# The last pair's softmax division moved from the probabilities to the mixed values

## The chip, the cores and the metric

The kernel runs on one NeuronCore of a Trainium2 chip. The metric is the device time of one execution in microseconds (us). Runs of the kernel before lie between 1137.45 and 1139.55 us, with a median of 1137.94 us over three.

## The reference

One decoder layer on 1024 tokens of width 1024, all in float32. RMSNorm of x feeds one combined input projection. Sixteen heads of width 64 follow: eight with a sliding window, sink logits and ALiBi (group A), and eight with forgetting attention (group B), whose logit gets `c[t] - c[s]` from a running sum of log forget gates. The output projection with a residual comes next, then RMSNorm and an MLP with a squared ReLU. What matters here is the end of group B:

```python
sc = jnp.where(causal, sc + bias, -jnp.inf)
p = jax.nn.softmax(sc, axis=-1)
return jnp.einsum('bhqs,bshd->bqhd', p, v)
```

A softmax is an exponential divided by its row sum. The row sum belongs to the query, so the division can stand on the probabilities (query by key) or on the mixed values (query by head width), with the same outcome up to rounding.

## The kernel before, in words

Products in float32 are made of three products of a rounded part and a remainder (`hi`, `lo`), and stationary tiles are 128 by 128. The order of work is: input projection and group A, then the eight group B heads in four pairs (p = 0 to 3), with the projections of the next pair and, from the third pair on, the first half of the output projection as fillers between them; then the second half of the output projection; then the MLP (`up`, `down`), which takes from about 503 us to the end.

A pair is made of eight units (`heads_b`), one for each head h and each pair of query blocks qp (256 queries). The order of qp is 0, 2, 1, 3 for the first head, and 1, 3, 0, 2 for the second head of the last pair. A unit has two parts:

- `scores_b` makes for each of its two query blocks i the negated logits (TensorE, tile `spb`), adds the forget bias and takes the running minimum (VectorE, L626, tile `sb`), and exponentiates (ScalarE, L632), which also gives the row sum.
- `mix_b`, called two units later (DEPTH = 2), turns the probabilities by TensorE transposes into `tpb` (L662), moves them to SBUF as a rounded part (ScalarE, L359, `pth`) and a remainder (VectorE, L360, `ptl`), and multiplies them with the values into `pvb`. The values' rounded part and remainder sit side by side in the stationary tile, so that `pvb` has two halves of 64 partitions, which must be added: ScalarE copies the upper half to `tmpb` (L677), and VectorE adds the lower half to it (L679, `mtb`).

For the first three pairs the probabilities stay undivided. The row sums are collected in `dn_b`, and `split_mix` divides the mixed values later, after a round through DRAM (L565). The last pair makes no such round trip: the probabilities themselves are divided, with a reciprocal of one column (L639) and a multiplication of the whole row of up to 1024 keys, on VectorE for query blocks 2 to 7 (L641) and on GpSimd for blocks 0 and 1 (L643). The result of `mix_b` is then split at once into `mh[7]` and `ml[7]`, the last operand of the output projection (`mix`, ScalarE L75 and VectorE L78).

Beside the last pair run `out_first` (first half of the output projection, one call for each of eight output columns, tiles `po`, `wos`, `xt`), `split_mix(6)` with its loads and stores, and the loads of the divided earlier pairs (`load_mix`, tile `mix<-mixs_d`). After the last unit's scores the program makes products of the first output column with operands 4 to 6, and, when the last unit is mixed, with operand 7.

The engines take their instructions in order. That order is written by a planner, which places instructions by priority on a simulated timeline: program order, with scores, preparations and weight splits pulled forward by an offset (`high_priority`), and fillers held behind the score of a given unit (`issue_after`, `PACE`). Buffers are rings: two for `tpb`, `pvb`, `spb`, `pth`, `ptl` and `mtb`, one for `tmpb`. A tile of a ring is taken again once all that touched it has ended.

Of the kernel before, what the change touches and what calls it, by code (L numbers as in the profile page):

```python
# [8 lines left out]
F32 = mybir.dt.float32  # L9
# [3 lines left out]
ALU = mybir.AluOpType  # L13
# [3 lines left out]
P = 128  # L17
# [4 lines left out]
HD = 64  # L22
# [31 lines left out]
def hybrid_layer(  # L54
# [13 lines left out]
    nc = tc.nc  # L68
# [11 lines left out]
    def rsqrt(pool, out, t, shape, tag):  # L80
# [12 lines left out]
    ident = cp.tile([P, P], F32, name="ident")  # L93
    nc.gpsimd.memset(ident, 0.0)
    nc.gpsimd.affine_select(
        out=ident, in_=ident, pattern=[[-1, P]], compare_op=ALU.not_equal,
# [16 lines left out]
    for i in range(2):  # L113
        nc.vector.tensor_tensor(
            out=gqk[:, i : i + 1], in0=vec[:, 2 * i : 2 * i + 1],
            in1=vec[:, 2 * i + 1 : 2 * i + 2], op=ALU.mult,
# [487 lines left out]
    def scores_b(p, qp, h):  # L604
        q1, k1, k2, cb = heads[p, "q"][h], heads[p, "k1", h], k2_of[h], heads[p, "cb", h]
        probs = []
        for i in (2 * qp, 2 * qp + 1):
            nk = (i + 1) * P
            pr = ap2.tile(
                [P, S if i > 3 else 512], F32, tag="s" if i > 3 else "u", name="sb",  # L610
                bufs=NS if i > 3 else NU,
            )
            nm = ap2.tile([P, 4], F32, tag="nm", name="nmb", bufs=4)
            dn = ap2.tile([P, 4], F32, tag="dn", name="dnb", bufs=4)
            qs = q1[:, i * P : (i + 1) * P]
            for c in range((nk + 511) // 512):
                n = min(512, nk - c * 512)
                ne = max(n, 256)
                ks = slice(c * 512, c * 512 + ne)
                sp = pa.tile([P, 512], F32, tag="sc", name="spb", bufs=2)  # L620
                last = (c + 1) * 512 >= nk
                mm(sp[:, :ne], qs, k1[:, ks], True, False)
                mm(sp[:, :ne], qs, k2[:, ks], False, not last)
                if last:
                    pe = mm(sp[:, n - P : n], ident_b, mask_b, False, True)
                nc.vector.tensor_tensor_reduce(  # L626
                    out=pr[:, c * 512 : c * 512 + n], in0=sp[:, :n],
                    in1=cb[:, c * 512 : c * 512 + n], scale=1.0,
                    scalar=3e38 if c == 0 else nm[:, 0:1],
                    op0=ALU.add, op1=ALU.min, accum_out=nm[:, c : c + 1],  # L630
                )
            nc.scalar.activation(  # L632
                pr[:, :nk], pr[:, :nk], AF.Exp, scale=-1.0, bias=nm[:, c : c + 1],
                accum_out=dn_b[p % 2][:, h, i : i + 1] if p < 3 else dn[:, 0:1],
            )
            probs.append(pr)
            if p < 3:
                continue
            nc.vector.reciprocal(dn[:, 1:2], dn[:, 0:1])  # L639
            if i > 1:  # L640
                nc.vector.tensor_scalar_mul(pr[:, :nk], pr[:, :nk], dn[:, 1:2])  # L641
            else:
                nc.gpsimd.tensor_tensor(  # L643
                    out=pr[:, :nk], in0=pr[:, :nk],
                    in1=dn[:, 1:2].to_broadcast([P, nk]), op=ALU.mult,
                )
        marks.append(pe.ins)
        return probs

    def mix_b(probs, p, qp, h):  # L650
        r = slice(h * HD, (h + 1) * HD)
# [23 lines left out]
                mm(pvo, st, lv[:, :, 1 - par, :], False, diag and par == 1)  # L675
        tmp = ap2.tile([HD, 512], F32, tag="cmb", name="tmpb", bufs=1)
        nc.scalar.copy(tmp[:, :256], pv[HD:, :256])  # L677
        mt = ap2.tile([P, 256], F32, tag="mt", name="mtb", bufs=2)
        nc.vector.tensor_tensor(out=mt[r, :], in0=pv[:HD, :256], in1=tmp[:, :256], op=ALU.add)  # L679
        ms = slice(qp * 256, (qp + 1) * 256)  # L680
        if p < 3:
            nc.sync.dma_start(mix_d[4 + p, r, ms], mt[r, :])
# [562 lines left out]
```

## Time and profile before

| | us |
|---|---|
| median of three runs | 1137.94 |
| lowest, highest | 1137.45, 1139.55 |
| the profiled execution | 1135.57 |
| its span, first to last instruction | 1133.8 |
| TensorE busy (share of the span) | 1105.2 (97%) |
| VectorE busy | 767.8 (68%) |
| ScalarE busy | 574.4 (51%) |
| GpSimd busy | 383.4 (34%) |

The granted clock of TensorE is 0.998 of full speed over the span. Busy time of TensorE counts a matmul to its modelled end, and neighbours overlap: a group's mean of one is longer than the distance from one matmul to the next. Idle time in square brackets is that of the instruction's engine just before it, with the instruction that ended it. Line numbers are those of the kernel before; L71, L75 and L78 are helpers (`mm`, and the two halves of `split`), so tiles say what they work on. PE is TensorE, PEld its weight loads, DVE VectorE, ACT ScalarE, POOL GpSimd.

### The profile page before, as it was taken

The page shows a single profiled execution, that of the slowest core. Times are in us where ns is not written, and L with a number is a line of the kernel's source. Part 1 is how long each engine was busy: PE and PEld are TensorE (multiplying, and loading weights), DVE is VectorE, ACT ScalarE, POOL GpSimd, SP SyncE. Part 2 cuts the span into 40 slices and gives each one's busy share as a digit, 9 for nine tenths or more (in the row PEclk, how much of TensorE's full clock was granted, in tenths as well). Part 3 has the DMA queues.
Part 4 walks back from the last instruction along what each step waited for, and adds up shares of the span by engine and source line. Part 5 has one row for each costly group of instructions (what it writes and reads, how often), then busy time and mean ns, then how long its engine had stood idle before and what let it go on. Part 6 is the DMA issues. An engine that isn't in the chain of part 4 may idle for free.

```text
span 1133.8 us, 15566 instructions
## 1 busy us (share of the span) xinstructions
PE 1105.2 (97%) x5551; PEld 937.0 (83%) x5551; DVE 767.8 (68%) x1307; ACT 574.4 (51%) x1013; POOL 383.4 (34%) x342
## 2 busy tenths in 40 slices
PE   9999999989999999999999999999999999999998
PEld 8999987888997887787888887888888888888876
DVE  7476665766558577798867677856575877674493
ACT  5567567666557666545454534344443433333330
POOL 5751513345324634133332322222222222231241
PEclk9999999999999999999999999999999999999999
DMA  9311301355307647363554544335699786665441
GB/s 314 117 43 29 94 20 54 94 170 167 105 27 294 196 166 258 124 231 130 186 195 168 194 149 154 141 119 200 227 391 347 265 303 233 230 232 183 167 149 38
DMA packets 95710, 195.68 MB, mean 173 GB/s; under 512 B 7136, under 2 KB 19088, under 8 KB 95632
## 3 DMA queue, kind: packets, MB, share of 16 engines
q1 hardware_dynamic: 95488, 194.66, 49.0%
q8 instruction: 44, 0.72, 0.3%
q14 instruction: 34, 0.28, 0.1%
q10 hardware_dynamic: 144, 0.02, 0.0%
HBM read 141.61 MB, written 53.04 MB: 172 GB/s over the span
## 4 chain that ended last, share of the span: by engine, by line
PE 75%; DVE 9%; DMA 6%; issue 5%; POOL 3%; ACT 2%; SPq 0%; DVEq 0%; POOLq 0%; ACTq 0%
PE pd L71 27%; PE pu L71 26%; PE ps L71 6%; PE po L71 5%; PE qps L71 3%; DMA mixr<-mix_d 2%; PE pvb L71 2%; PE spb L71 2%; DVE ptl L360 1%; DMA h_d<-h 1%; PE sp L71 1%; PE tpb L662 1%; DVE sb L626 1%; POOL qkb L267 1%; DVE ss L241 1%
## 5 line engine op out<-in xcount | busy, mean ns | idle before, releaser
L71 PE MATMUL pd<-hx,wx 128*128 128x512 f32 x1344 | 306.8, 391 | 2.4 <-POOL wx L78 2.4
L71 PEld LDWEIGHTS pd<-hx,wx 128*128 128x128 f32 x1344 | 253.4, 189 | 55.7 <-POOL wx L78 2.8
L71 PE MATMUL pu<-bh,wu 128*128 128x512 f32 x896 | 281.9, 395 | 0.8 <-ACT bh L858 0.8
L71 PEld LDWEIGHTS pu<-bh,wu 128*128 128x128 f32 x896 | 168.3, 188 | 41.9 <-ACT bh L858 1.3
L71 PE MATMUL pu<-bl,wu 128*128 128x512 f32 x448 | 176.8, 395 | 0.1
L78 POOL TENSOR_TENSOR wx<-wda,wx 128x1024 fp32r<-128x1024 f32 x28 | 85.0, 3038 | 221.5 <-ACT wx L75 193.9
L75 ACT CAST hx<-hr 128x1024 fp32r<-128x1024 f32 x56 | 59.0, 1054 | 181.0 <-PE pd L71 175.8
L78 DVE TENSOR_TENSOR hx<-hr,hx 128x1024 fp32r<-128x1024 f32 x56 | 76.0, 1364 | 81.4 <-ACT hx L75 81.2
L71 PE MATMUL ps<-wh,xh 128*128 128x384 f32 (+1 forms) x320 | 110.3, 345 | 0.3 <-ACT qkb L582 0.3
L71 PE MATMUL ps<-wh,xl 128*128 128x384 f32 (+1 forms) x320 | 109.1, 342 | 0.0
L71 PE MATMUL ps<-wl,xh 128*128 128x384 f32 (+1 forms) x320 | 109.0, 341 | 0.0
L71 PEld LDWEIGHTS pu<-bl,wu 128*128 128x128 f32 x448 | 84.2, 188 | 21.0 <-DVE bl L78 0.8
L71 PE MATMUL po<-mix,wos 128*128 128x512 f32 x384 | 96.6, 398 | 2.3 <-ACT mix L75 0.8
L78 POOL TENSOR_TENSOR wu<-wus,wu 128x512 fp32r<-128x512 f32 x32 | 46.6, 1458 | 134.3 <-ACT wu L75 128.5
L71 PEld LDWEIGHTS po<-mix,wos 128*128 128x128 f32 x384 | 70.0, 188 | 17.6 <-ACT mix L75 1.5
L75 ACT CAST wu<-wus 128x512 fp32r<-128x512 f32 x64 | 39.0, 618 | 83.9 <-PE pu L71 75.7
L78 POOL TENSOR_TENSOR wu<-wur,wu 128x512 fp32r<-128x512 f32 x32 | 45.9, 1436 | 88.4 <-ACT wu L75 88.4
L926 DVE TENSOR_TENSOR ht<-hb 128x512 f32<-128x512 f32 x32 | 21.8, 722 | 67.0 <-ACT hb L981 67.0
L78 POOL TENSOR_TENSOR wl<-wr,wh 128x384 fp32r<-128x384 f32 (+1 forms) x47 | 50.0, 1075 | 50.0 <-ACT wh L75 38.6
L360 DVE TENSOR_TENSOR ptl<-tpb,pth 128x512 fp32r<-128x512 f32 (+1 forms) x80 | 50.2, 632 | 19.6 <-ACT pth L359 18.5
L75 ACT CAST wx<-wda 128x1024 fp32r<-128x1024 f32 x56 | 58.3, 1044 | 6.9 <-DMA wda<-in_w_d_dram 6.6
L71 PEld LDWEIGHTS ps<-wh,xh 128*128 128x128 f32 x320 | 60.4, 189 | 1.4 <-ACT qkb L582 0.6
(213 smaller groups left out, 2056.3 us busy)
## 6 DMA issues: line engine op xcount, KB each, us to landing
wda<-in_w_d_dram SPq DMA_DIRECT2D x34, 1024.0 KB, 8.5
hr<-hid_d SPq DMA_DIRECT2D x56, 512.0 KB, 5.8
wur<-in_w_u_dram SPq DMA_DIRECT2D x32, 512.0 KB, 4.4
hid_d<-ht SPq DMA_DIRECT2D x16, 1024.0 KB, 4.3
hid_d<-hb SPq DMA_DIRECT2D x16, 768.0 KB, 3.6
mixs_d<-mixs SPq DMA_DIRECT2D x14, 512.0 KB, 3.5
mix<-mixs_d SPq DMA_DIRECT2D x7, 1024.0 KB, 8.2
wr<-in_w_b_dram SPq DMA_DIRECT2D x32, 192.0 KB, 2.6
```

The costliest lines, as they stand in the source:

```text
L71: return nc.tensor.matmul(out, lhsT, rhs, start=start, stop=stop)
L75: hi_eng.copy(hi, src)
L78: lo_eng.tensor_tensor(out=lo, in0=src, in1=hi.bitcast(F32), op=ALU.subtract)
L241: nc.vector.tensor_reduce(out=ss, in_=sq[:, : n * w].rearrange("p (g d) -> p g d", d=HD), axis=AX.X, op=ALU.add,)
L267: nc.gpsimd.tensor_tensor(out=xt, in0=xt, in1=rv[:, t].unsqueeze(2).to_broadcast([P, na, HD]), op=ALU.mult)
L360: nc.vector.tensor_tensor(out=lo[:, cols], in0=pt[:, cols], in1=hi[:, cols].bitcast(F32), op=ALU.subtract)
L626: nc.vector.tensor_tensor_reduce(out=pr[:, c * 512 : c * 512 + n], in0=sp[:, :n], in1=cb[:, c * 512 : c * 512 + n], scale=1.0, scalar=3e38 ...
L662: nc.tensor.transpose(tp[:, c0 : c0 + P], probs[qi][:, kb * P : (kb + 1) * P], ident)
L926: eng.tensor_tensor(out=out, in0=a, in1=b, op=ALU.subtract)
```

## The change

In the last pair the row sums now go to `dn_b[1]`, as they do for the other pairs, and the probabilities are left undivided: sixteen one-column reciprocals, twelve multiplications on VectorE and four on GpSimd are gone. In `mix_b` of the last pair, after ScalarE's copy of the upper half, VectorE makes the reciprocals of the unit's two row-sum columns at once. Two TensorE transposes turn each of them, repeated over 64 columns, into a tile of 64 partitions by 128 queries in the right half of the same `pvb` tile, where nothing stood. VectorE adds the two halves into `tmpb` in place, and in a second instruction multiplies `tmpb` with the turned reciprocals into `mtb`. The eight units of the last pair do this; the other pairs are as before.

```diff
-            dn = ap2.tile([P, 4], F32, tag="dn", name="dnb", bufs=4)
...
-                accum_out=dn_b[p % 2][:, h, i : i + 1] if p < 3 else dn[:, 0:1],
+                accum_out=dn_b[p % 2][:, h, i : i + 1],
             )
             probs.append(pr)
-            if p < 3:
-                continue
-            nc.vector.reciprocal(dn[:, 1:2], dn[:, 0:1])
-            if i > 1:
-                nc.vector.tensor_scalar_mul(pr[:, :nk], pr[:, :nk], dn[:, 1:2])
-            else:
-                nc.gpsimd.tensor_tensor(
-                    out=pr[:, :nk], in0=pr[:, :nk],
-                    in1=dn[:, 1:2].to_broadcast([P, nk]), op=ALU.mult,
-                )
...
         nc.scalar.copy(tmp[:, :256], pv[HD:, :256])
+        if p == 3:
+            rd = ap2.tile([P, 2], F32, tag="dn", name="dnr", bufs=4)
+            nc.vector.reciprocal(rd, dn_b[1][:, h, 2 * qp : 2 * qp + 2])
+            for j in range(2):
+                nc.tensor.transpose(
+                    pv[:HD, (2 + j) * P : (3 + j) * P], rd[:, j : j + 1].to_broadcast([P, HD]),
+                    ident,
+                )
+            nc.vector.tensor_tensor(
+                out=tmp[:, :256], in0=pv[:HD, :256], in1=tmp[:, :256], op=ALU.add
+            )
         mt = ap2.tile([P, 256], F32, tag="mt", name="mtb", bufs=2)
-        nc.vector.tensor_tensor(out=mt[r, :], in0=pv[:HD, :256], in1=tmp[:, :256], op=ALU.add)
+        both = (pv[:HD, 256:], tmp[:, :256], ALU.mult) if p == 3 else (
+            pv[:HD, :256], tmp[:, :256], ALU.add
+        )
+        add = nc.vector.tensor_tensor(out=mt[r, :], in0=both[0], in1=both[1], op=both[2])
```

## Rows read from the trace of the kernel before

**Rows 1.** The head of the page and its part 1: busy time of an engine, its share of the span, and its instructions.

```profile
span 1133.8 us, 15566 instructions
PE 1105.2 (97%) x5551; PEld 937.0 (83%) x5551; DVE 767.8 (68%) x1307; ACT 574.4 (51%) x1013; POOL 383.4 (34%) x342
```

**Rows 2.** Busy time of each engine by stretch, over the last pair's last two thirds up to the last products of the first output column. Columns: stretch and its length, then the busy time of PE, PEld (weight loads), DVE, ACT and POOL with the instructions in brackets, the granted clock of TensorE (1.00 is full speed), the DMA share and GB/s.

```profile
419.00:433.00 14.00, 13.96 (x72) 11.29 (x71) 11.87 (x30) 8.61 (x19) 7.18 (x8) 1.00 0.59 191
433.00:439.10 6.10, 6.05 (x43) 5.25 (x42) 5.90 (x13) 4.42 (x13) 2.67 (x5) 1.00 0.87 291
439.10:445.00 5.90, 4.78 (x35) 3.80 (x33) 3.99 (x11) 3.80 (x10) 3.92 (x8) 1.00 0.84 328
445.00:449.75 4.75, 4.03 (x24) 3.32 (x23) 3.74 (x11) 3.10 (x7) 0.00 (x0) 1.00 0.74 267
449.75:452.00 2.25, 2.25 (x13) 1.92 (x14) 0.44 (x1) 0.00 (x0) 0.00 (x0) 1.00 0.13 29
452.00:456.00 4.00, 3.62 (x28) 3.02 (x28) 2.78 (x5) 2.90 (x6) 0.74 (x4) 1.00 0.35 130
456.00:460.20 4.20, 3.84 (x27) 3.00 (x25) 3.33 (x7) 3.19 (x7) 0.38 (x2) 1.00 0.00 0
460.20:463.45 3.25, 2.17 (x7) 1.09 (x7) 2.38 (x5) 1.24 (x3) 0.00 (x0) 1.00 0.00 0
```

**Rows 3.** Groups of instructions by form, VectorE alone, between 380 and 466 us. Columns: line, engine, operation, out<-in, shapes, count | busy us, mean ns of one | idle time before them.

```profile
L679 DVE TENSOR_TENSOR mtb<-pvb,tmpb 64x256 f32<-64x256 f32 x13 | 5.4, 412 | 5.1 <-ACT tmpb L677 4.9
...
L641 DVE TENSOR_SCALAR sb<-sb,dnb 128x1024 f32<-128x1024 f32 x2 | 2.7, 1373 | 0.0
...
L641 DVE TENSOR_SCALAR sb<-sb,dnb 128x896 f32<-128x896 f32 x2 | 2.6, 1318 | 0.1
L639 DVE RECIPROCAL dnb<-dnb 128x1 f32<-128x1 f32 x16 | 2.2, 149 | 0.8 <-ACT sb L632 0.8
...
L641 DVE TENSOR_SCALAR sb<-sb,dnb 128x640 f32<-128x640 f32 x2 | 2.1, 1042 | 0.0
...
L641 DVE TENSOR_SCALAR sb<-sb,dnb 128x384 f32<-128x384 f32 x2 | 1.6, 823 | 0.0
...
L641 DVE TENSOR_SCALAR sb<-sb,dnb 128x512 f32<-128x512 f32 x2 | 1.5, 770 | 0.0
...
L641 DVE TENSOR_SCALAR sb<-sb,dnb 128x768 f32<-128x768 f32 x2 | 1.2, 613 | 0.0
```

**Rows 4.** The timeline of all engines in order of time, where the divisions of query blocks 6, 7 and then 0, 1 of head 1 lie. Columns: start us, length us, engine, line, operation, out<-in, shapes, count [idle before <-releaser].

```profile
432.69 1.74 DVE L641 TENSOR_SCALAR sb<-sb,dnb 128x896 f32<-128x896 f32 x1
...
434.23 0.48 ACT L359 CAST pth<-tpb 128x384 fp32r<-128x384 f32 x1
...
434.40 1.29 POOL L817 TENSOR_TENSOR xt<-xt,pc 128x512 f32<-128x512 f32 x1 [0.46 <-ACT pc L816]
...
434.53 2.00 DVE L641 TENSOR_SCALAR sb<-sb,dnb 128x1024 f32<-128x1024 f32 x1
...
436.45 0.54 DVE L360 TENSOR_TENSOR ptl<-tpb,pth 128x384 fp32r<-128x384 f32 x1
...
437.24 0.27 DVE L626 CUSTOM_DVE_ANT_0 sb<-spb,cb 128x128 f32<-128x128 f32 x1
...
438.95 0.97 POOL L643 TENSOR_TENSOR sb<-sb,dnb 128x128 f32<-128x128 f32 x2 [2.97 <-DVE dnb L639]
```

**Rows 5.** The timeline of TensorE alone at four transposes whose weights have 64 columns, with the next instruction behind them; columns as in rows 4.

```profile
380.14 0.60 PE L288 MATMUL ptk<-ident,qkb 128*64 128x128 f32 x4
380.50 0.36 PE L71 MATMUL pvb<-ptl,vb 128*128 128x256 f32 x1
```

**Rows 6.** The timeline of all engines at the end of the last pair; columns as in rows 4.

```profile
457.98 0.42 DVE L679 TENSOR_TENSOR mtb<-pvb,tmpb 64x256 f32<-64x256 f32 x1
...
458.44 0.37 ACT L677 COPY tmpb<-pvb 64x256 f32<-64x256 f32 x1
...
458.45 0.19 PEld L71 LDWEIGHTS pvb<-pth,vb 128*128 128x128 f32 x1
...
461.03 0.28 PE L71 MATMUL pvb<-ptl,vb 128*128 128x256 f32 x1
...
461.80 0.42 DVE L679 TENSOR_TENSOR mtb<-pvb,tmpb 64x256 f32<-64x256 f32 x1 [0.72 <-ACT tmpb L677]
...
462.71 0.50 PE L71 MATMUL po<-mix,wos 128*128 128x512 f32 x1 [0.83 <-ACT mix L75]
...
463.45 1.21 PE L71 MATMUL po<-mix,wos 128*128 128x512 f32 x4 [0.24 <-DVE mix L78]
```

**Rows 7.** The chain of waits that ended last, between 405 and 466 us, in order of time. Columns: start us, length us, what.

```profile
441.55 8.15 DMA mix<-mixs_d
...
449.75 1.68 PE po L71 x6
```

**Rows 8.** The timeline of all engines at two of the copies of the upper half of a mixed tile, each with the last product before it; columns as in rows 4.

```profile
433.81 0.28 PE L71 MATMUL pvb<-ptl,vb 128*128 128x256 f32 x1
...
434.73 0.37 ACT L677 COPY tmpb<-pvb 64x256 f32<-64x256 f32 x1
...
439.12 0.28 PE L71 MATMUL pvb<-ptl,vb 128*128 128x256 f32 x1
...
440.13 0.37 ACT L677 COPY tmpb<-pvb 64x256 f32<-64x256 f32 x1
```

## The prediction

> **What bounds the kernel now.** I read the page's part 1 first: TensorE is busy for 1105.2 of 1133.8 us, and VectorE for 767.8 [rows 1]. So time can be won only where TensorE stands idle, and lost wherever work is put on it. The change touches only the last pair, so I cut that stage into stretches [rows 2]. The reader is to see two regimes there. From 419 to 439.1 us TensorE misses 0.04 and 0.05 us only; at the end of that VectorE is as full, 5.90 of 6.10 us. From 439.1 to 463.45 us TensorE idles in five of the six stretches: 1.12, 0.72, 0.38, 0.36 and 1.08 us, 3.66 us in all. In this tail the fillers have run out, and the chain "transpose, copy, remainder, product" of the last units sets the pace, with one transfer beside it, the load of a mixed operand, which the chain of waits shows for 8.15 us up to 449.70 [rows 7]. The groups of VectorE then say what the divisions cost [rows 3], and the timelines where they stand in the way [rows 4] and what the stage ends on [rows 6].
>
> **What the change removes.** On VectorE: 12 multiplications, by form 2.7 + 2.6 + 2.1 + 1.6 + 1.5 + 1.2 = 11.7 us, and 16 reciprocals, 2.2 us [rows 3]. On GpSimd: four multiplications, two of which take 0.97 us together [rows 4]. In the full stretch before 433 us this buys nothing, since TensorE has no idle time there to give back; the price of these edits is nothing, and the cover is TensorE's own queue. It counts at 432.69 to 436.53 us: two multiplications of 1.74 and 2.00 us keep VectorE from the remainder (L360) at 436.45, whose input ScalarE had finished at 434.23 + 0.48 = 434.71. Without them that remainder can start at about 434.71, so it and what is queued behind it, the logits of the last head's first query blocks (L626 at 437.24) among them, move forward by 436.45 - 434.71 = 1.74 us [rows 4]. The bounds are 0 (what comes next waits for something else) and 3.74 us (both multiplications). I take 1.74, because the row names the input that is late next.
>
> GpSimd's two go at 438.95 us; 0.97 us on the way from the logits to the transposes of query blocks 0 and 1. These lie within the same part of the tail, behind the same VectorE instructions; I count 0 for them, with 0.97 as the other end.
>
> **What it adds on TensorE.** Sixteen transposes with 64 weight columns. Four such take from 380.14 to the next instruction at 380.50, 0.09 us each [rows 5], so 16 x 0.09 = 1.44 us. As long as the pair runs in the full stretch each counts in whole: the units mixed there are about the first four, 8 x 0.09 = 0.72 us. Those of the last four fall where TensorE idles for 3.66 us [rows 2] and I count 0. The bounds are 0 and 1.44 us; if each stood alone to its end, 0.60 - 3 x 0.09 = 0.33 us by the same row, it would be 16 x 0.33 = 5.3 us, which belongs to the slow rival.
>
> **What it adds on VectorE.** Eight two-column reciprocals, at least 149 ns each by the one-column row, 1.2 us, and eight more additions or multiplications of 64 x 256 at 412 ns [rows 3], 3.3 us. VectorE's balance is 13.9 - 4.5 = 9.4 us less work. But the second instruction of a unit lies on the path twice. First, the result of the third last unit (L679, 457.98 + 0.42 = 458.40 us) lets go of the `tmpb` buffer and of a `pvb` tile: the next copy starts at 458.44 and the last unit's first weight load at 458.45 [rows 6]. One more instruction of 0.42 us before that release moves both by 0.42 us. Second, the last unit: last product at 461.03, addition at 461.80, products of operand 7 at 462.71 and 463.45 [rows 6]; nothing runs beside it that could hide 0.42 us. Together 0.84 us. The bounds: 0.42 (the planner puts other work at the first place) and 1.53 us (at the first place a remainder of 0.69 us comes between the two; 0.42 + 0.69 + 0.42).
>
> **The added waits.** The transposes wait for the reciprocal on VectorE; its input is there since the exponential, two units before, so only the queue of VectorE counts, and behind the waiting transposes stands all of TensorE. The addition on VectorE waits for the transposes, and behind it stand the remainders of the next blocks, for which TensorE's products wait. The multiplication waits for the addition only. DMA queues: no DMA is added or moved in the program; the loads and stores on the SP queue keep their order unless the planner changes it.
>
> **The sum**, against the profiled execution of 1135.57 us (span 1133.8): -1.74 + 0.72 + 0.84 = -0.18 us, that is 1135.4. This execution lies 2.4 us under the median of the runs, 1137.94; the difference carried over, the forecast is 1137.7 us. The least that a measurement of this kernel can tell from no change is about 0.2%, 2.3 us: faster is under 1135.7, slower above 1140.2.
>
> **The rivals.**
>
> *The tail closes up (faster).* With 9.4 us less on VectorE the planner starts the last units' scores earlier by both multiplications, 3.74 us, and the fillers sink into TensorE's idle time, with 0.72 us of it before the operand's load gone as well. For it: VectorE is full from 433 to 439.1 us, and the tail holds 3.66 us of idle TensorE [rows 2]. Against it: the rows show only 1.74 us until another input is late. Time: -(3.74 + 0.72) + 0.72 + 0.84 = -2.9, 1135.0 us.
>
> *The transfer is late instead (no gain).* TensorE's products at 449.75 us wait for the load that lands at 449.70 [rows 7], and their place in the queue is fixed; TensorE coming there 1.74 us earlier only waits longer. The load hangs on transfers, not on the divisions. Against it: the mixing of the last units can be put ahead of these products. Time: +0.84 with the transposes absorbed in that wait, 1138.8; with them, +1.56, 1139.5 us.
>
> *TensorE stands behind the turned reciprocals (slower).* The transposes write the same `pvb` tile that ScalarE's copy reads, and in program order they come after the copy. If the planner keeps that order as a wait and puts them straight behind the unit's last product, TensorE stands until the copy has ended: 434.73 + 0.37 - (433.81 + 0.28) = 1.01 us and 440.13 + 0.37 - (439.12 + 0.28) = 1.10 us [rows 8], 1.05 us a unit. For four units in the full stretch that is 4.2 us: -0.2 + 4.2 = +4.0, 1141.9 us. It decides from three units on (3 x 1.05 - 0.2 = 3.0 us). Against it: the planner sees the copy's length and has other products to put between, as long as fillers last. The Trainium skill, in "PSUM — Partial Sum Buffer" under "PSUM bank collisions raise a hardware error", asks that TensorE's writes be kept apart from the reads of ScalarE and VectorE by bank and group of 32 partitions, at other addresses of the bank too. By its group rule the copy (partitions 64 to 127) and the transposes (0 to 63) may overlap and this rival falls to nothing, and only VectorE's addition, from partitions 0 to 63, has to follow the transposes; by its simpler rule, whole banks, the rival stands. No row here shows a TensorE write beside a read of the same tile.
>
> **How the numbers follow.** The forecast gets 0.42, the closing tail 0.24, the late transfer 0.18, the standing TensorE 0.16. Faster: most of the closing tail, whose 1135.0 lies just past the bound (0.20), and a little of the forecast's upper end (1.74 could be 3.74): 0.25. Slower: nearly all of the standing TensorE and the upper ends of the 0.84 and 0.72: 0.20. Within 0.2%: 0.55. The range goes from 1134.6, just beyond the closing tail, to 1141.4, with three to four standing units.
>
> **What would show it right or wrong.** Right: 433 to 439.1 us on VectorE without L641 and its remainder about 1.7 us earlier against the start of the last scores; sixteen transposes of the reciprocal at 0.09 us apart from their neighbours; two instructions of 0.41 us per unit where L679 stood; 0.4 us more between the last product of the last unit and the products of operand 7. Wrong: idle time of TensorE released by the copy or the reciprocal before these transposes (the slower rival); products of operands 4 to 6 waiting for `mix<-mixs_d` by clearly more than 0.72 us (the transfer); idle time between 439 and 463 us much under 3.66 us with the stage ending 3 us sooner (the closing tail). A changed order in the stages before 380 us, which I count as unchanged, would overturn the sum altogether.

## The result, and the profile after

The kernel after takes 1141.25 us (median of 13 runs, 1137.36 to 1143.35), the kernel before 1138.26 us in the same session: a ratio of 1.0030, 95% interval 1.0018 to 1.0042, slower by 0.3%. The forecast was 1137.7 us, no change. The profiled execution of the kernel after is one of 1141.44 us. The head of its page and part 1 [rows 1]:

```profile
span 1139.7 us, 15589 instructions
...
PE 1108.0 (97%) x5567; PEld 944.0 (83%) x5567; DVE 762.2 (67%) x1295; ACT 574.8 (50%) x1013; POOL 385.4 (34%) x338
```

VectorE lost 5.6 us of work and TensorE got its sixteen transposes, but the span grew. To find where, I cut the last pair at products of TensorE: the last of the projections (`ps`), the last score (`spb`), the last value product (`pvb`), the first of operand 7's second half and the last of the output projection (`po`). In us, from end to end in the first and last line and from start to start in the two others:

| from, to | profiled before | three other traces of before | after |
|---|---|---|---|
| last `ps` to last `spb` | 103.4 | 103.5 to 103.7 | 102.1 |
| last `spb` to last value product | 16.1 | 15.1 | 16.3 |
| last value product to second half of operand 7 | 1.68 | 1.67 to 1.68 | 3.81 |
| last `ps` to last `po` of the output projection | 161.6 | 160.2 to 160.4 | 163.1 |

The other three are traces of the same kernel, and of it with a few instructions put in that change nothing before the last wait (runs e1, e7, e14). They show that the profiled execution of the kernel before was not typical in one place: its wait of 0.72 us for `mix<-mixs_d` [rows 7] does not occur in them. A fifth trace of that kernel, e6 (with the cut that is explained below), is not in the table: its pair takes 163.5 us, with a wait of 1.94 us for `pth` and a fall of the clock, 1.7 us, at 371 to 376 us.

**The relief is there.** From the timelines of TensorE and VectorE in the kernel after (columns as in [rows 4]), the first line's two products and VectorE in between:

```profile
344.76 0.33 PE L71 MATMUL ps<-wh,xl 128*128 128x384 f32 x1
...
435.13 1.23 DVE L565 TENSOR_TENSOR mixr<-mixr,mixn 128x512 f32<-128x512 f32 x1 [1.23 <-POOL xt L821]
...
436.95 0.55 DVE L360 TENSOR_TENSOR ptl<-tpb,pth 128x384 fp32r<-128x384 f32 x1
...
446.96 0.23 PE L71 MATMUL spb<-mask_b,ident_b 128*128 128x128 bf16 x1
```

Counted from the end of the last `ps`, the remainder (L360) stands 2.8 us earlier than in [rows 4] (436.95 - 345.09 = 91.86 against 436.45 - 341.76 = 94.69), and the last score 1.3 us earlier. VectorE, no longer full, waits there for GpSimd.

**The end of the pair gives more than that back.** The timeline of the kernel after, the last three units [rows 6]:

```profile
459.43 0.42 DVE L676 TENSOR_TENSOR tmpb<-pvb,tmpb 64x256 f32<-64x256 f32 x1 [0.23 <-PE pvb L672]
459.84 0.69 DVE L360 TENSOR_TENSOR ptl<-tpb,pth 128x512 fp32r<-128x512 f32 x1
460.56 0.42 DVE L683 TENSOR_TENSOR mtb<-pvb,tmpb 64x256 f32<-64x256 f32 x1
461.01 0.37 ACT L666 COPY tmpb<-pvb 64x256 f32<-64x256 f32 x1 [1.28 <-DVE mtb L683]
...
461.12 0.36 PE L71 MATMUL pvb<-pth,vb 128*128 128x256 f32 x1 [1.32 <-DVE mtb L683]
...
463.29 0.28 PE L71 MATMUL pvb<-ptl,vb 128*128 128x256 f32 x1
463.71 0.40 ACT L75 CAST mix<-mtb 64x256 fp32r<-64x256 f32 x1 [1.40 <-DVE mtb L683]
464.13 0.37 ACT L666 COPY tmpb<-pvb 64x256 f32<-64x256 f32 x1
...
464.55 0.14 PEld L672 LDWEIGHTS pvb<-ident,dnr 128*64 128x64 f32 x2 [0.21 <-ACT tmpb L666]
...
465.07 0.42 DVE L676 TENSOR_TENSOR tmpb<-pvb,tmpb 64x256 f32<-64x256 f32 x1 [0.51 <-PE pvb L672]
465.47 0.69 DVE L872 TENSOR_TENSOR h<-po,h 128x512 f32<-128x512 f32 x1
466.19 0.42 DVE L683 TENSOR_TENSOR mtb<-pvb,tmpb 64x256 f32<-64x256 f32 x1
466.64 0.40 ACT L75 CAST mix<-mtb 64x256 fp32r<-64x256 f32 x1 [2.14 <-DVE mtb L683]
...
467.10 9.11 PE L71 MATMUL po<-mix,wos 128*128 128x512 f32 x30 [1.66 <-ACT mix L75]
```

In the third last unit a remainder of 0.69 us stands between the addition and the multiplication, and TensorE waits 1.32 us for the multiplication to let go of `pvb`. In the last unit the copy starts 0.84 us after the start of the last product (0.37 before), because ScalarE first converts the unit before it; the addition comes 0.94 us behind the copy (0.40 before), because the transposes wait for the copy and the addition for the transposes; and from the addition to the product there are 2.03 us (0.91 before), because the eviction `h` (0.70 with its gap) and the multiplication (0.42) stand between: 0.47 + 0.54 + 1.12 = 2.13 us. The copy of the last unit in the kernel before, whose neighbours are in [rows 6]:

```profile
461.40 0.37 ACT L677 COPY tmpb<-pvb 64x256 f32<-64x256 f32 x1 [1.24 <-PE pvb L71]
```

**Then the clock falls.** Stretches of 2 us of the kernel after, columns as in [rows 2]:

```profile
460.00:462.00 2.00, 0.88 (x7) 0.91 (x8) 1.11 (x3) 0.94 (x3) 0.22 (x2) 1.00 0.00 0
462.00:464.00 2.00, 1.36 (x9) 0.85 (x7) 1.56 (x4) 0.60 (x2) 0.16 (x1) 1.00 0.00 0
464.00:466.00 2.00, 1.27 (x5) 0.62 (x5) 1.35 (x3) 0.48 (x2) 0.00 (x0) 1.00 0.00 0
466.00:468.00 2.00, 0.91 (x2) 0.64 (x3) 1.18 (x4) 1.12 (x2) 0.00 (x0) 0.91 0.00 0
468.00:470.00 2.00, 2.00 (x5) 1.16 (x5) 1.27 (x2) 1.12 (x2) 0.53 (x1) 0.50 0.00 0
470.00:472.00 2.00, 2.00 (x8) 1.54 (x8) 1.06 (x2) 0.84 (x2) 0.75 (x1) 0.74 0.75 284
```

TensorE is busy for 4.42 of the 8 us up to 468, and then works at 0.50, the level of 1.2 GHz, for a while: (0.09 + 0.50 + 0.26) x 2 = 1.7 us lost.

**A stall ahead of the change.** The kernel after also loses time where its order of instructions is that of the kernel before. First its stretches at 130 us, columns as in [rows 2]; then a wait of the SP queue (us in total, times, longest us) and a line of TensorE's timeline, last the same line in the kernel before:

```profile
120.00:130.00 10.00, 9.77 (x62) 9.16 (x60) 3.38 (x14) 2.60 (x5) 2.96 (x3) 1.00 0.22 69
130.00:140.00 10.00, 7.99 (x41) 7.69 (x42) 6.00 (x18) 6.78 (x21) 5.96 (x6) 0.83 0.51 165
```

```profile
SPq L562 <- DMA mix_d<-mta: 3.0, 1, 3.0
```

```profile
132.01 0.50 PE L71 MATMUL pv<-pth,va 128*128 128x512 f32 x1 [2.24 <-ACT pth L359]
```

```profile
128.84 0.50 PE L71 MATMUL pv<-pth,va 128*128 128x512 f32 x1 [0.64 <-ACT pth L359]
```

The load `mixr<-mix_d` waits 3.0 us on the SP queue for the stores before it (0.7 in a trace without the stall, e3), behind it are the weight loads that ScalarE waits for, and TensorE waits 2.24 us (0.64 before), with the clock at 0.83 behind it. The packet records show a fetch of instructions (16 KB, 0.88 us) falling among the stores' packets. The last sixteen of their 256 packets come only as it ends, 1.1 us after the others, at up to 84 ns instead of 27. Wait and clock together are some 3.3 us (2.24 - 0.64 + 1.7), as much as the whole difference; the runs below ask whether it is the cause.

### The profile page after: what moved, and what is told of

It is laid out like the page before. It is cut to its first block, busy times and chain, and to the rows that moved or that the text cites. A ratio compares the mean times of both kernels' runs of the same rounds, so it can differ in the third digit from the quotient of the medians.

```text
span 1139.7 us, 15589 instructions
## 1 busy us (share of the span) xinstructions
PE 1108.0 (97%) x5567; PEld 944.0 (83%) x5567; DVE 762.2 (67%) x1295; ACT 574.8 (50%) x1013; POOL 385.4 (34%) x338
## 4 chain that ended last, share of the span: by engine, by line
PE 80%; DVE 6%; DMA 5%; issue 4%; POOL 2%; ACT 2%; SPq 0%; DVEq 0%; POOLq 0%; ACTq 0%
PE pu L71 26%; PE pd L71 26%; PE ps L71 10%; PE po L71 5%; PE qps L71 3%; PE pvb L71 2%; PE spb L71 2%; DMA mixr<-mix_d 2%; PE tpb L651 1%; PE sp L71 1%; DMA h_d<-h 1%; DVE ptl L360 1%; DVE sb L625 1%; PE pv L71 1%; PE tpa L519 1%
## 5 line engine op out<-in xcount | busy, mean ns | idle before, releaser
L78 POOL TENSOR_TENSOR wx<-wda,wx 128x1024 fp32r<-128x1024 f32 x28 | 90.3, 3227 | 216.3 <-ACT wx L75 216.3
L78 DVE TENSOR_TENSOR hx<-hr,hx 128x1024 fp32r<-128x1024 f32 x56 | 72.5, 1299 | 85.7 <-ACT hx L75 83.5
L78 POOL TENSOR_TENSOR wu<-wus,wu 128x512 fp32r<-128x512 f32 x32 | 48.9, 1529 | 131.4 <-ACT wu L75 131.4
L360 DVE TENSOR_TENSOR ptl<-tpb,pth 128x512 fp32r<-128x512 f32 (+1 forms) x80 | 50.3, 634 | 19.4 <-ACT pth L359 18.0
```

The lines of the kernel that those rows point to most:

```text
L78: lo_eng.tensor_tensor(out=lo, in0=src, in1=hi.bitcast(F32), op=ALU.subtract)
L360: nc.vector.tensor_tensor(out=lo[:, cols], in0=pt[:, cols], in1=hi[:, cols].bitcast(F32), op=ALU.subtract)
```

## The experiments

Each kernel was timed against the kernel before on the same chip. "Cut" means that the warming matmuls, products at the start of the program that nobody reads, are cut into more instructions. "Clock share" is the mean of (1 - granted clock) x span over a kernel's 8 to 13 runs (30 to 35 in a set of the kernel before); its standard error is 0.4 to 1.0 us, in those sets 0.3 to 0.4. "Last wait" is the third line of the table above.

| run | median us | ratio, 95% interval | clock share us | last wait us |
|---|---|---|---|---|
| before (four sets) | 1137.4 to 1137.8 | | 4.6 to 5.3 | 1.7 |
| after | 1141.25 | 1.0030, 1.0018 to 1.0042 | 7.3 | 3.8 |
| e1 before again | 1136.93 | 0.9988, 0.9974 to 1.0002 | 4.5 | 1.7 |
| e2 after again | 1141.58 | 1.0025, 1.0005 to 1.0044 | 6.7 | 3.8 |
| e3 divisions out | 1134.42 | 0.9971, 0.9959 to 0.9984 | 4.3 | 1.7 |
| e4 additions in | 1142.70 | 1.0047, 1.0025 to 1.0069 | 8.0 | 3.8 |
| e5 cut, after | 1139.58 | 1.0021, 1.0006 to 1.0036 | 6.9 | 3.8 |
| e6 cut, before | 1135.29 | 0.9979, 0.9962 to 0.9996 | 4.8 | 1.7 |
| e7 longer code, before | 1136.79 | 0.9991, 0.9973 to 1.0008 | 5.1 | 1.7 |
| e8 cut, end mended | 1137.80 | 0.9989, 0.9971 to 1.0007 | 4.9 | 2.3 |
| e9 cut, last wait filled | 1138.51 | 0.9997, 0.9984 to 1.0010 | 3.7 | 3.8 |
| e10 cut, one unit | 1137.81 | 1.0001, 0.9985 to 1.0017 | 5.5 | 1.7 |
| e11 cut, six units | 1137.42 | 0.9995, 0.9981 to 1.0008 | 5.7 | 1.7 |
| e12 cut, `h` held | 1140.14 | 1.0019, 1.0006 to 1.0033 | 6.7 | 3.1 |
| e13 last wait filled | 1138.52 | 1.0017, 1.0006 to 1.0028 | 3.8 | 3.8 |
| e14 before, filled | 1136.85 | 0.9998, 0.9983 to 1.0012 | 4.4 | 1.7 |
| e15 mended, filled | 1137.30 | 0.9998, 0.9986 to 1.0011 | 4.8 | 2.3 |
| e16 cut, mended, filled | 1135.12 | 0.9979, 0.9967 to 0.9990 | 3.6 | 2.3 |

**Both kernels again, and each half of the change alone.** e1 and e2 are the two kernels unchanged. e3 leaves the last pair's division out altogether; e4 is the kernel before with all that the change adds, and divides twice: it has the lines that e3 takes out of the kernel after.

```diff
-            rd = ap2.tile([P, 2], F32, tag="dn", name="dnr", bufs=4)
-            nc.vector.reciprocal(rd, dn_b[1][:, h, 2 * qp : 2 * qp + 2])
...
-        add = nc.vector.tensor_tensor(out=mt[r, :], in0=both[0], in1=both[1], op=both[2])
+        nc.vector.tensor_tensor(out=mt[r, :], in0=pv[:HD, :256], in1=tmp[:, :256], op=ALU.add)
```

> The kernel before, unchanged, for a second profile and as a measure of how far two series of one kernel lie apart. Theory of the tail: the granted clock stays at full speed between 440 and 530 us, as in the first profile, and only stretches before 380 us may show a fall; the first products of operand 7 follow the last mixing product by about 1.7 us again. Theory of chance (falls of the clock strike any profile of either kernel): a fall between 440 and 530 us shows here in about every second profile. Ratio to the kernel before 1.000 within 0.001 by both.

> The changed kernel, unchanged, for a second profile. Theory of the tail: TensorE idles again by 1.3 us for the released mixed tile, by about 0.8 and 1.7 us for operand 7, and the clock falls to its lower level for some 4 us just behind, near 467 us, and again near 518 us; ratio 1.002 to 1.004. Theory of TensorE load (the sixteen transposes are the cost): idle times may differ, the ratio stays at 1.0013. Theory of chance: the two falls are not there, and the profiled time comes down by about 3 us.

> The division of the last pair is left out altogether: probabilities undivided, no reciprocal, no transposes, no multiplication of the mixed values, so the last pair's part of the output is not divided. What remains is the relief alone. Theory of the tail: the last mixing product comes 1.3 to 2 us earlier than in the kernel before, measured from the end of the last projection, the operand 7 products follow by 1.7 us, no fall of the clock; 1 to 2 us faster than before, ratio 0.998 to 0.999. Theory of TensorE load: 1.4 us faster than the changed kernel and no more, ratio about 1.0015 to 1.002. My prediction's relief term: -1.74 us, ratio 0.9985.

> The additions alone: the probabilities are divided as before, and the mixed values are multiplied once more, by turned reciprocals of an earlier pair's sums, so the last pair's part of the output is divided twice. Theory of the tail: the end of the pair waits as in the changed kernel (3.8 us from the last mixing product to the second half of operand 7) and nothing is given back: 1.3 us or more slower than the changed kernel, ratio 1.004 to 1.006. Theory of TensorE load: +1.4 us against before, ratio 1.0013. My prediction's terms: +0.72 + 0.84 = +1.56 us, ratio 1.0014.

The difference repeats. The fall of the clock behind the pair repeats too, in e2 at 470 us, but the one forecast near 518 us does not. e1 missed its forecast in one point: its clock falls at 513 to 520 us, for 3.4 us of loss. Falls that start between 511 and 521 us stand in the traces of both kernels (e1, e7; after, e4, e5), so falls there say nothing of the change; only those at 460 to 480 us are used below.

The removal alone gives 0.29%, 3.3 us, and the additions alone cost 0.47%, 5.3 us. In e3 the last score ends 101.6 us after the last `ps`, 1.8 us sooner than in the profiled execution before. Removal and additions sum up to 2.0 us; the whole change costs 3.0, and the intervals are wider than that difference. The trace of e4 has the stall at 130 us and that of e3 has not, so the two do not part the end of the pair from the stall.

**Is it the stall at 130 us?** The same columns of warming matmuls, cut into more instructions, move the later fetches:

```diff
-    for _ in range(NWARM):
-        mm(qps[7], warm[:, :P], warm, True, True)
+    for _ in range(3 * NWARM):
+        mm(qps[7][:, :170], warm[:, :P], warm[:, :170], True, True)
```

e7 is the kernel before with sixteen unread products behind its last:

```diff
                     finish(n, ps)
+                    if i == len(STEPS) - 1:
+                        for _ in range(16):
+                            mm(ps[0][:, :64], w[:, 0, 0, :P], x[:, 0, 0, :64], True, True)
```

> The kernel after, with the eight warming matmuls of 512 columns at the very start cut into 24 of 170 columns: the same columns, but 16 more matmuls and weight loads in TensorE's code. The order of every engine is otherwise that of the kernel after. The packets of instructions on queue q8 are fetched as TensorE's code is used up (16 KB in about 22 us, some 250 instructions), so 32 instructions more at the start bring each later fetch forward by about 2.5 us. Theory 'fetch': the loss lies at 123 to 140 us, where a 16-KB fetch of instructions falls among the packets of the stores mix_d<-mta, the load mixr<-mix_d waits 3.0 us for them and TensorE 2.2 us for pth, and the clock falls to 0.83 for 10 us (2.2 - 0.6 + 1.7 = 3.3 us). Then the stall is gone here: TensorE waits for pth at about 130 us no more than 0.7 us, the clock stays at 1.00 in 130 to 140 us, and the median is 1138.0 us (1136.8 to 1139.2). Theory 'tail': the loss lies in the end of the last pair, so 1141.4 us as for the kernel after (1140.5 to 1142.3). A third case: the shifted fetch meets other transfers, and a stall shows at another place.

> The same cut of the warming matmuls in the kernel before: the control for the run above. Theory 'fetch': the kernel before has hardly any of that stall to lose, so 1137.3 us (1136.3 to 1138.3), within 1 us of the kernel with the change and the same cut. Theory 'tail': 1137.3 us too, but 4 us under the kernel with the change and the same cut. If the cut by itself gains or costs time, it shows here alone.

> The kernel before with 16 matmuls of 64 columns more at the very end of TensorE's code, after its last product, into a bank that has been read already: nobody reads them, and they run beside the last evictions. All orders are otherwise those of the kernel before; TensorE's code is only longer at its end, as that of the kernel after is longer in its middle. Does the length of the code alone bring the stall at 130 us? If yes: the wait for pth of over 1.7 us at about 130 us and 1140 to 1141.5 us. If no: 0.4 to 0.7 us of wait and 1137.6 us (1136.6 to 1138.4). Theory 'tail' has 1137.6 us too.

The stall goes, as the theory 'fetch' said, and the clock is at 1.00 there. A line of TensorE's timeline in e5:

```profile
129.78 0.50 PE L71 MATMUL pv<-pth,va 128*128 128x512 f32 x1 [0.90 <-ACT pth L359]
```

But the time doesn't follow: with the cut the kernels differ by 1139.58 - 1135.29 = 4.3 us, no less than without. By its median e5 is a miss for both theories, halfway between them. The cut gains some 0.2% in the kernel before; what by was not followed up. e7's longer code brings no stall (0.59 us of wait), nor is it in the traces of e13 and e15, which have the added instructions without the cut. So the change doesn't need the stall to be slower: with the cut the loss is there without it. In the pair without the cut it is part of the traces (after, e2 and e4 have it, the kernel before and its variants have not), and how much of the 3.0 us it is there stays open. What brings it on stays open too. By the packet records a fetch falls among these stores in the kernel before, e1, e3, e7, e13, e14 and e15 as well, but there only the last 8 packets come late, and the load goes out before them; and in e3 and the kernel before it starts 0.3 us behind the first packet, just as in e2 and e4, which stall. With the cut the fetch starts ahead of the stores, and none of their packets is held back to its end.

**Is it the end of the pair?** e12 (with the cut) puts the eviction `h` behind the multiplication; e8 also puts the transposes ahead of ScalarE's copy.

```diff
-            nc.vector.tensor_tensor(out=h[:, cs], in0=ps[c], in1=h[:, cs], op=ALU.add)
+            with tc.issue_after(last_mix[0]) if dt == 0 else nullcontext():
+                nc.vector.tensor_tensor(out=h[:, cs], in0=ps[c], in1=h[:, cs], op=ALU.add)
```

The second edit of e8:

```diff
-        nc.scalar.copy(tmp[:, :256], pv[HD:, :256])
...
                     ident,
                 )
+            nc.scalar.copy(tmp[:, :256], pv[HD:, :256])
```

> The kernel after with the cut warming matmuls and one exchange: the addition h of the first output column's eviction (0.69 us on VectorE), which stands between the addition and the multiplication of the last unit, is put behind the multiplication. Every other order is the same. Theory 'tail': 0.69 us off the 3.81 us between the last product and the second half of operand 7, so 0.7 us faster than the neighbour without the exchange (1139.6), 1138.9 us and ratio 1.0014; if the clock then no longer falls, 1.7 us more, 1137.2 us and 1.000. Theory 'something else delays operand 7': no change, 1139.6 us.

> The kernel after with the cut warming matmuls, and two edits in the last pair's end: the transposes of the reciprocals stand ahead of ScalarE's copy of the upper half in program order, and the additions h of the first output column's eviction are held behind the last unit's multiplication. To be compared with the same kernel without the two edits (the run of this call). Theory 'tail': between the last product of the last unit and the second half of operand 7 go 3.81 us in the kernel after; without h (0.72) and without the transposes' wait for the copy (0.4 of it) 2.7 us remain, and if the clock no longer falls at 467 to 472 us another 1.7 us come back: 1.1 to 2.8 us faster than its neighbour. Theory 'fetch': the tail has little to give, 0 to 1.1 us faster. If the transposes ahead of the copy make the copy wait (they need the reciprocal), it may lose 0.2 us a unit.

e12's last wait is 0.7 us shorter, as forecast, and its median stays where e5's is: half a hit. Its one trace shows no fall of the clock at 460 to 480 us, but its runs lose as much clock as e5's. e8 mends both places. The last unit in its timeline:

```profile
461.47 0.28 PE L71 MATMUL pvb<-ptl,vb 128*128 128x256 f32 x1
...
461.58 0.38 PE L673 MATMUL pvb<-ident,dnr 128*64 128x128 f32 x2
...
462.00 0.37 ACT L677 COPY tmpb<-pvb 64x256 f32<-64x256 f32 x1 [1.16 <-PE pvb L673]
462.41 0.42 DVE L678 TENSOR_TENSOR tmpb<-pvb,tmpb 64x256 f32<-64x256 f32 x1 [0.95 <-ACT tmpb L677]
462.86 0.42 DVE L685 TENSOR_TENSOR mtb<-pvb,tmpb 64x256 f32<-64x256 f32 x1
...
463.76 0.50 PE L71 MATMUL po<-mix,wos 128*128 128x512 f32 x1 [1.32 <-ACT mix L75]
```

The transposes follow straight behind the last product, nothing stands between copy, addition and multiplication, and the wait of 1.32 us for the third last unit is gone too. (The wait of 1.32 us in the last line is another, the one before operand 7's second half, 1.66 us in the kernel after.) It is 1.8 us faster than e5 in the median, as forecast; by the ratios, taken in the same session, it is 0.32% faster, 0.9989 against 1.0021. It loses 2.0 us less to the clock, with a standard error of 1.2.

e10 and e11 divide some of the units as before; `cond` stands for all but blocks 6 and 7 of head 1 in e10, and for the last two units in e11:

```diff
+                accum_out=dn[:, 0:1] if p == 3 and cond else dn_b[p % 2][:, h, i : i + 1],
...
+            if not (p == 3 and cond):
+                continue
+            nc.vector.reciprocal(dn[:, 1:2], dn[:, 0:1])
...
```

> The change in one of the eight units alone, with the cut warming matmuls: only head 1's query blocks 6 and 7 keep their probabilities undivided (the two long multiplications before the late remainder are theirs); the other seven units are divided as before. It adds two transposes and one instruction of VectorE for the unit, and the two last units are as in the kernel before. Theory 'relief and tail': the relief of 1.3 us or more (up to the 3.2 us that leaving all divisions out gave) stays and the tail's loss goes: 1.1 to 2.5 us below the kernel before with the same cut (1135.3), ratio to the kernel before 0.9957 to 0.997, and no fall of the clock at 460 to 475 us. Theory 'TensorE load': the sixteen transposes are the price; with two of them left the result is the same. If the relief needs all divisions to go, 1135.3 us and 0.998.

> The change in six of the eight units, with the cut warming matmuls: the last two units (head 1's query blocks 0, 1 and 4, 5) are divided as in the kernel before, so the end of the pair has one instruction of VectorE per unit again and no transposes of reciprocals behind the last products. Theory 'tail': the loss sits in those two units, so this one is as fast as or faster than the kernel before with the same cut: 1133.8 to 1135.8 us, ratio 0.9965 to 0.9985. Theory 'TensorE load' (twelve transposes and their waits in the full stretch cost up to 3 us): 1137 to 1139 us, ratio 1.000 to 1.002.

Both fell short. e11's 0.9995 lies between what the two theories expected, and e10's 1.0001 is well above its own. Their last wait is 1.7 us again, as the theory 'tail' has it, but the third last unit (blocks 6 and 7) is undivided in both, and with its second instruction TensorE's wait for `mtb` stays, 1.24 and 1.32 us: only half of the end was as before. For TensorE's load there is little room: with twelve transposes e11's last pair takes 160.5 us from the last `ps` to the last `po`, with that wait in it, where the kernel before takes 160.2 to 161.6 (163.5 in e6). Why e10 with two transposes takes 161.6 us was not followed up.

**Is it the clock?** Unread products fill the last wait and can bring no operand earlier (eight after the change, four in e14):

```diff
-    out_products(po_first, w, [7])
...
+            idle = pa.tile([P, 512], F32, tag="sc", name="idle", bufs=2)
+            with tc.issue_after(half.ins):
+                for _ in range(NIDLE):
+                    mm(idle, w[0][:, 2, :], mh[6][:, :512], True, True)
...
```

> The kernel after with the cut warming matmuls, and eight products of 512 columns that nobody reads on TensorE between the first and the second half of operand 7's products, where it stands idle for 1.66 us (8 x 0.21 = 1.7 us; they write a bank of the scores' ring that is free by then). The other orders are those of the same kernel without them, but for one addition h of VectorE. They can bring the second half no earlier; what they can change is the clock. Theory 'tail with the clock': the fall to 0.50 at 466 to 468 us follows TensorE's idle time, 1.32 + 0.59 + 1.66 us in the ten us before it. With one of the three filled the clock stays at 1.00 there and the kernel gains up to 1.7 us on its neighbour without them: 1138 us, ratio to the kernel before about 1.0006. If the fall has nothing to do with the idle time it comes all the same: 1139.6 us, ratio 1.002, or up to 0.3 us more if the eight run over the end of the wait.

> The kernel after with nothing but the eight unread products between the two halves of operand 7 (the warming matmuls as they were). Theory 'clock after the waits': over the runs of one kernel the part of the span that the granted clock takes away, (1 - clock) x span, is 7.3 and 6.7 us in the two sets of the kernel after, 6.9 and 6.7 us in the two others that end the pair like it, 4.5 to 5.3 us in the kernel before, and 3.7 us in the one whose last wait was filled. So some 2 of the 3 us are clock. Then here (1 - clock) x span is under 5.3 us, the ratio to the kernel before 1.0005 to 1.0015, 1138.5 to 1139.5 us. Theory 'waits alone': the eight products give nothing, ratio 1.0025 to 1.003 and about 7 us of clock. Theory 'fetch': the stall at 130 us is still there in its profile whichever it is.

> The control: the kernel before with four unread products (0.85 us) in its own wait of 0.83 us between the two halves of operand 7. Both theories expect little: the kernel before has no fall of the clock at that place in any of its traces, so ratio 0.999 to 1.001 and 4.5 to 5.5 us of clock. If it gains 0.15% or more, filling waits helps any kernel, and the run above says nothing of the change.

First stretches of e5 and then the same of e9, where TensorE's order differs by the eight products alone (columns as in [rows 2]):

```profile
462.00:464.00 2.00, 0.79 (x3) 0.48 (x3) 1.18 (x4) 1.12 (x2) 0.00 (x0) 1.00 0.00 0
464.00:466.00 2.00, 1.50 (x6) 0.94 (x5) 1.29 (x2) 1.29 (x2) 0.87 (x1) 0.78 0.00 0
466.00:468.00 2.00, 2.00 (x6) 1.58 (x5) 1.24 (x2) 0.66 (x2) 0.40 (x1) 0.50 0.94 325
```

```profile
462.00:464.00 2.00, 1.69 (x7) 1.04 (x7) 1.18 (x3) 1.36 (x3) 0.47 (x1) 1.00 0.00 0
464.00:466.00 2.00, 2.00 (x11) 1.63 (x10) 1.75 (x2) 0.38 (x2) 1.33 (x1) 1.00 0.68 266
466.00:468.00 2.00, 2.00 (x10) 1.68 (x9) 0.69 (x1) 0.54 (x1) 0.00 (x0) 1.00 0.46 133
```

Then stretches of e13, which differs from the kernel after in TensorE's order by the eight products alone, and TensorE's timeline there:

```profile
464.00:466.00 2.00, 2.00 (x10) 1.45 (x8) 1.50 (x4) 0.57 (x2) 0.00 (x0) 1.00 0.00 0
466.00:468.00 2.00, 1.68 (x7) 0.88 (x7) 1.17 (x3) 1.36 (x3) 0.21 (x1) 1.00 0.00 0
468.00:470.00 2.00, 2.00 (x9) 1.63 (x10) 1.86 (x2) 0.54 (x1) 1.60 (x1) 1.00 0.64 262
470.00:472.00 2.00, 2.00 (x10) 1.64 (x10) 0.84 (x2) 0.62 (x1) 0.00 (x0) 1.00 0.62 166
```

```profile
462.07 0.28 PE L72 MATMUL pvb<-ptl,vb 128*128 128x256 f32 x1
...
464.03 2.02 PE L72 MATMUL idle<-mix,wos 128*128 128x512 f32 x8
465.89 1.63 PE L72 MATMUL po<-mix,wos 128*128 128x512 f32 x5
```

The wait is as long as ever (465.89 - 462.07 = 3.82 us), and the clock holds. With the cut, e5 against e9, the clock share falls from 6.9 to 3.7 us and the ratio from 1.0021 to 0.9997; neither trace has the stall at 130 us. Without it the share falls from 7.3 and 6.7 us to 3.8 and the ratio from 1.0030 and 1.0025 to 1.0017, just above the forecast, but that pair is not clean: the trace of e13 lacks the stall at 130 us, which the theory 'fetch' had expected there, and with it the clock's fall at that place, so part of its gain may be the stall's. The control moves by nothing. The fall stands at 460 to 480 us in all four traces of kernels that end the pair like the kernel after (after, e2, e4, e5), and in none of the five of the kernel before and its variants (before, e1, e6, e7, e14). These are one trace for each kernel, and e12 shows what that is worth: its trace has no fall, its runs have the clock share of e5's.

**The version meant to win.** e15 and e16 join the mended end and six filling products, without and with the cut.

> The kernel after with three edits in the last pair's end and the warming matmuls as they were: transposes of the reciprocals ahead of ScalarE's copy, the addition h behind the multiplication, and six unread products (1.3 us) in the last wait. Theory 'tail and clock': the relief of 1.3 to 1.7 us is kept, the end of the pair is as long as in the kernel before, and the clock does not fall there: 1136.0 to 1137.5 us, ratio 0.998 to 1.000, and no more than 5 us of clock. Theory 'fetch': the stall at 130 us remains a loss of 3 us whatever the end of the pair does: 1139 us or more.

> The same three edits with the cut warming matmuls: the version meant to beat both kernels. The cut gave the kernel before 0.2% (2.1 us, interval 0.4 to 4.3), the mended end 2.5 us in the profile's stage of the last pair against the kernel after with the same cut. 1134.5 to 1136.5 us, ratio 0.9965 to 0.9985. If it is no faster than the kernel before with the cut (1135.3), the relief is worth no more than what the added instructions take.

Both came within their forecasts. e15 is level with the kernel before. e16 is 0.21% faster than it, but the cut alone (e6) gives the kernel before the same 0.21%. No version of the change was found that beats the kernel before by its own doing.

## Why the prediction was wrong

**Right: relief and transposes.** 1.74 us were taken for the relief; e3 shows 1.8 us at the last score and 1.75 at the remainder itself (435.13 - 342.19 = 92.94 against 94.69 us after the last `ps`); in the kernel after the same remainder came 2.8 us earlier. In the six traces that have the whole change with the third last unit as it was (after, e2, e5, e9, e12, e13) the last score ends 101.9 to 102.7 us after the last `ps`, 0.2 to 1.1 us later than in e3: that is what the transposes and the rest of the additions take there, forecast at 0.72. The net of -1.02 us was measured as -1.3 in the profiled execution, and as -0.7 to -1.6 in these six.

**Wrong: the term of 0.84 us for the end of the pair.** Measured it is 1.2 us up to the last value product (against 15.1 us in the traces without the transfer's wait) and 2.13 us behind it, 3.3 us in all. The first place was priced at 0.42 us; its upper bound, 0.42 + 0.69 with a remainder between the two instructions, is what happened. At the last unit I added the length of one instruction to a chain whose other links I took as they were. But an instruction more changes who is next on each queue: ScalarE's copy came behind the conversion of the unit before, the transposes behind the copy, the multiplication behind `h`. Only 0.42 of the 2.13 us is the added instruction.

**Missing: the clock.** No term stood for it. Over the runs the kernel after and the three others with its full end lose 6.7 to 8.0 us to the clock, the kernel before 4.6 to 5.3: some 2 us more. In the pair with the cut, where no trace has the stall, it is 6.9 against 4.8, 2.1 of a difference of 4.3 us; without the cut part of it may be the fall behind the stall at 130 us. That the idle time in the last wait brings on the fall at 460 to 480 us is borne out by e9, whose filling products leave the wait as it is: the fall is gone, and the clock share is 3.2 us lower, with a standard error of 1.1. One fall is 1.7 us; whether more than that one goes isn't shown. The stage itself, with a fall of 1.7 us taken out where it lies in it, takes 161.4 to 163.0 us in after, e2, e5, e9 and e13, against 160.2 to 160.4 before: 1.0 to 2.8 us more. With the 2 us of clock this is 3 to 5 us, about what was measured (3.0 without the cut, 4.3 with it); a finer split the runs do not give.

**Luck.** The range went up to 1141.4 us, but for three to four units with TensorE standing behind the copy, which did not happen; that 1141.25 lies in it is no merit of the terms.

**The rivals.** The late transfer is wrong: its wait isn't longer but gone. The closing tail is wrong as a result, though VectorE did come free. Standing behind the turned reciprocals was half right: the first rows of this tile's record and its waits in the kernel after are

```profile
L672 PE MATMUL pvb<-ident,dnr x16: 270/272/297, 428.3 to 464.7; 128*64 128x128 f32 x16
...
  ACT tmpb L666: 0.2, 1
who waited for it (us, times):
  DVE tmpb L676: 5.0, 6
```

TensorE stood behind the copy in one unit of eight, for 0.2 us, and not for 1.05 us in four: the planner found other products to put between. VectorE waited for the transposes, 5.0 us in six units; on the way to operand 7 lies the last of these waits (0.51 us), and before it the one of 0.23 us in the third last unit. On the sentence weighed from the Trainium skill ("PSUM — Partial Sum Buffer", "PSUM bank collisions raise a hardware error"): the transposes into partitions 0 to 63 start at 464.55, 0.05 us after the copy of 64 to 127 has ended, and in e8 the copy waits for the transposes. So in these kernels the order follows the whole tile. It is an order that the program asks for; whether the chip would have allowed the overlap by partitions, no run here shows.

The sum was also made against an execution with a wait of 0.72 us that the four other traces of that kernel lack. No term of the sum used it, but the rival of the late transfer hung on it.

## What to carry to other kernels

At the end of a stage, where nothing is left to put between, price an added instruction by walking the chain again with every queue's new neighbours (what is now ahead of the copy, what the planner slides in between two halves), not by its length. Ask after any lengthened wait of TensorE what the clock does behind it: here some 2 us of the loss were not the wait but the clock, and products nobody reads, put into the wait, brought them back (e9 against e5). An operation moved from an engine with slack to the last unit's chain has to be shorter there than the relief elsewhere.

## What the hardware showed unasked

TensorE's clock fell to 0.50 not in the waits but at their end or behind it: in the kernel after 0.5 us after the last wait, in e5 and e2 1.9 and 2.0 us after it, in e4 as it ended. There it cost its 1.7 us on work: in the kernel after TensorE is busy without a gap while the clock is low. A fetch of 16 KB of instructions that falls among small stores (64 KB, packets of 512 B) came with a load behind them that waited 3.0 instead of 0.7 us, and with it, over two more queues, TensorE lost 1.6 us at 130 us; moved by 32 instructions at the start of the program the fetch did no harm. In other traces a fetch falls among the same stores and does none either. The runs of one kernel lie 3 to 9 us apart (e5: 1136.2 to 1143.9), mostly more than the change is worth; so the last pair was compared by its stretches in the traces, and the whole kernel by intervals.
